# A hybrid decoder layer on one core: attention operands laid out and loaded in pieces, bias copied by head, MLP in groups of 704 columns with seven products

## The chip, the core and the metric

The kernel runs on one core of a Trainium2 chip. A core has five engines with queues of their own: TensorE (PE) for matmuls, VectorE (DVE), ScalarE (ACT), GpSimd (POOL), and SyncE (SP), which here issues the DMAs. They run side by side and wait for each other by semaphores. The metric is the device time of one execution in microseconds, as the median of several runs.

## What is computed

One decoder layer, for a prompt of 2048 tokens and 64 sample tokens, that is 2112 columns, with a model width of 1024. Cut to what matters here:

```
def decoder_layer(x, ...):
    n = rms_norm(x, ln1_g)
    proj = n @ w_in                                   # 1024 x 3360
    q, k, v = head_rms(...), head_rms(...), ...       # 8 heads x 64
    att = dilated_attention(q, k_ctx, v_ctx, ..., bias_table)   # 3 dilations
    rw, wkv_T, shift_T = rwkv7_time_mix(proj[..., 1536:], ...)
    mixed = concatenate([att, rw], -1)
    h = x + mixed @ w_out                             # 1024 x 1024
    m = rms_norm(h, ln2_g)
    y = h + square(relu(m @ w_mlp1)) @ w_mlp2         # 1024 x 4096 x 1024
```

## The kernel before, in words

Data lie transposed, features on the 128 partitions and tokens as columns. Every float32 operand is split in a high part (a copy by ScalarE to `fp32r`, helper `act`, line 184) and a low part (the difference, by VectorE, helper `tt`, line 181), and a product is three matmuls: high by high, high by low, low by high. Line 175 is the helper `stt` (scalar_tensor_tensor), line 178 `tsc`. A scheduler fixes each engine's order ahead of time from the program's order and its own estimates; tile pools with a number of buffers decide when a load may start.

The stages, by the span: up to 1208 us the projections in four groups of 512 tokens and the recurrence; 1230 to 1640 us the dilated attention, four head pairs `p` with three dilations `b` and four groups each; to 1923 us the sample tokens' attention and the output projection; then the MLP.

*Bias.* `bias_vectors` (line 458) is a generator that one loop of the projections pumps. It makes, per head, a vector by distance, and line 477 copies it to `bvD`, 128 rows for each head, four heads in one DMA. The attention reads skewed tiles `bt` of it (line 1012).

*Attention operands.* `transposed_out` writes the high and low parts of q and k of each head pair to DRAM (`qhD`, `qlD`, `khD`, `klD`, lines 831 and 832). `kq_load` (line 994) builds for each head `ty` of a pair the tiles `kst` (k high, twice), `qst` (q high above q low) and `klo` (k low, twice), 128 x 2048, from six loads of 64 x 2048 at line 1004. It is called for the first pair ahead of the attention and for the next pair at `b` = 1. Values come as tiles `vt` (line 1023). The scores are the matmuls of lines 1066 and 1067, the weighted sums those of 1091. `merge` weighs the three dilations; its weights go through DRAM (`wD`, `wrow`, lines 1166 and 1169), and a matmul with them is line 1176.

*W_out.* The 2112 columns are taken in eight tiles of `NC_` = 264; `mix_panel` (line 1306) loads and splits the mixed input (`mr`), line 1421 loads x into `h` (tile by tile of one large buffer that keeps all columns), line 1431 has the 192 matmuls of a tile, and the result is added to `h`, from which `square_sums` (line 1391) makes the norms of 128 columns at a time.

*MLP.* Two halves of 1088 and 1024 columns, in matmul chunks of 364, 362, 362 and of 512, 512. `normed(half)` scales `h` by the norms and splits it into `mmh` and `mml`. For each of eight blocks `fc` of 512 hidden units come the first layer (line 1488), relu and square, and the second layer (line 1505), which is added to `h`. `normed(1)` is called ahead of the last second layer of the first half. `mpanel` loads and splits weight panels of 128x512, with four buffers.

## Time and profile before

| | |
|---|---|
| median of 3 runs | 3410.0 us (3407.44 to 3411.9) |
| profiled execution, its own time | 3415.77 us |
| its span | 3414.0 us |
| mean granted TensorE clock | 0.974 |
| TensorE busy | 3209.2 us, 94% |
| VectorE, ScalarE, GpSimd busy | 50%, 39%, 12% |
| DMA over the span | 107 GB/s, 364.73 MB |

Times of the profile are microseconds from the span's start. Durations come from one execution, which took 5.8 us more than the median. [...] The DMA share is the mean busy share of the core's sixteen DMA engines. A wait is put down to what came last. Single operations of one engine overlap a little in the records, so the time that one costs in a row of them is read from start to start.

### The profile page before, as it was taken

The numbers are of one execution on the slowest core, as the hardware profiler recorded it, in microseconds if no ns is written. First come the engines' busy times: TensorE is split into PE (matmuls) and PEld (weight loads), VectorE is DVE, ScalarE is ACT, GpSimd is POOL, SyncE is SP. The second block draws the span as 40 slices with busy tenths as digits, with TensorE's granted clock in tenths as the row PEclk, the third lists the DMA queues.
The fourth block names the chain that finished last, engine by engine and source line by source line (L and its number), as shares of the span: only waits on it lengthen the run. The fifth ranks groups of instructions, "written<-read, shape, count | busy, mean of one in ns | idle before, by whom it ended". The sixth has DMA issues, their size and how long they took to land.

```text
span 3414.0 us, 60201 instructions
## 1 busy us (share of the span) xinstructions
PE 3209.2 (94%) x23646; PEld 2791.4 (82%) x23646; DVE 1713.4 (50%) x3951; ACT 1326.7 (39%) x3209; POOL 395.2 (12%) x713
## 2 busy tenths in 40 slices
PE   5959999999999979989899999999999999999999
PEld 5836877786788857878688899999999988888887
DVE  4635676677677525546554643333333633333333
ACT  4435564565455536657322322222222322222221
POOL 1003243342354100111000000000000000000000
PEclk9979999999999989999899999999999999999999
DMA  5445464465355495333776111111111211111112
GB/s 165 136 141 161 131 191 139 119 174 145 112 146 153 131 212 113 94 87 99 261 244 206 44 47 44 47 44 44 44 46 44 97 49 49 48 50 47 50 47 74
DMA packets 336968, 364.73 MB, mean 107 GB/s; under 512 B 112907, under 2 KB 226374, under 8 KB 333612
## 3 DMA queue, kind: packets, MB, share of 16 engines
q1 hardware_dynamic: 336684, 360.88, 36.5%
q8 instruction: 186, 3.05, 0.4%
q14 instruction: 98, 0.80, 0.1%
HBM read 286.20 MB, written 79.30 MB: 107 GB/s over the span
## 4 chain that ended last, share of the span: by engine, by line
PE 59%; DMA 6%; DVE 2%; SPq 1%; issue 1%; ACT 1%; POOL 1%; DVEq 0%; ACTq 0%; POOLq 0%
PE pm L1505 21%; PE pm L1488 21%; PE pwo L1431 4%; PE o L1091 2%; PE sc L1066 2%; PE pt L1084 2%; PE sc L1067 2%; PE pj L789 1%; DMA kst<-khD 1%; DMA vt<-vD 1%; DMA kv<-in_kc 1%; DMA mr<-mixA 1%; SPq L1421 1%; PE sc L1233 0%; DMA wD<-wh 0%
## 5 line engine op out<-in xcount | busy, mean ns | idle before, releaser
L184 ACT ACTIVATE wh<-wr 128x512 fp32r<-128x512 f32 (+1 forms) x472 | 294.3, 624 | 1027.5 <-PE pm L1505 582.3
L181 DVE TENSOR_TENSOR wl<-wr,wh 128x512 fp32r<-128x512 f32 (+1 forms) x472 | 325.9, 692 | 425.0 <-ACT wh L184 410.7
L1488 PE MATMUL pm<-mml,wh 128*128 128x512 f32 (+2 forms) x1280 | 452.5, 354 | 3.3 <-DVE mml L181 3.3
L1488 PE MATMUL pm<-mmh,wh 128*128 128x512 f32 (+2 forms) x1280 | 454.8, 356 | 0.4 <-ACT mmh L184 0.4
L1488 PE MATMUL pm<-mmh,wl 128*128 128x512 f32 (+2 forms) x1280 | 452.8, 354 | 0.0
L1505 PE MATMUL pm<-fh,wh 128*128 128x512 f32 (+2 forms) x1280 | 450.5, 355 | 0.0
L1505 PE MATMUL pm<-fh,wl 128*128 128x512 f32 (+2 forms) x1280 | 449.6, 353 | 0.0
L1505 PE MATMUL pm<-fl,wh 128*128 128x512 f32 (+2 forms) x1280 | 448.4, 352 | 0.0
L181 DVE TENSOR_TENSOR h<-pm,h 128x364 f32<-128x364 f32 (+1 forms) x320 | 190.5, 598 | 423.9 <-PE pm L1505 423.7
L1488 PEld LDWEIGHTS pm<-mml,wh 128*128 128x128 f32 x1280 | 241.0, 188 | 27.4 <-DVE mml L181 5.9
L1488 PEld LDWEIGHTS pm<-mmh,wl 128*128 128x128 f32 x1280 | 241.9, 189 | 22.5
L1505 PEld LDWEIGHTS pm<-fh,wl 128*128 128x128 f32 x1280 | 240.7, 188 | 22.4
L1488 PEld LDWEIGHTS pm<-mmh,wh 128*128 128x128 f32 x1280 | 241.4, 189 | 19.9 <-ACT mmh L184 0.9
L1505 PEld LDWEIGHTS pm<-fl,wh 128*128 128x128 f32 x1280 | 240.0, 188 | 21.5
L1505 PEld LDWEIGHTS pm<-fh,wh 128*128 128x128 f32 x1280 | 240.3, 188 | 19.2
L789 PE MATMUL pj<-wh,nh 128*128 128x256 f32 (+1 forms) x816 | 237.3, 292 | 7.5 <-ACT qn L184 3.5
L789 PE MATMUL pj<-wh,nl 128*128 128x256 f32 (+1 forms) x816 | 236.2, 290 | 1.0 <-DVE nl L181 0.9
L330 PE MATMUL pj<-nh,wh 128*128 128x512 f32 (+3 forms) x600 | 222.7, 375 | 13.2 <-ACT nh L184 9.9
L789 PE MATMUL pj<-wl,nh 128*128 128x256 f32 (+1 forms) x816 | 234.6, 288 | 0.0
L330 PE MATMUL pj<-nl,wh 128*128 128x512 f32 (+3 forms) x600 | 221.6, 370 | 3.9 <-DVE nl L181 3.8
L330 PE MATMUL pj<-nh,wl 128*128 128x512 f32 (+3 forms) x600 | 217.5, 365 | 0.0
L184 ACT ACTIVATE e<-e,st 128x256 f32<-128x256 f32 (+1 forms) x384 | 174.3, 455 | 106.3 <-DVE st L1069 104.4
(295 smaller groups left out, 6105.3 us busy)
## 6 DMA issues: line engine op xcount, KB each, us to landing
wr<-in_w SPq DMA_DIRECT2D x256, 256.0 KB
wr<-in_wr SPq DMA_DIRECT2D x120, 256.0 KB
wr<-in_wq SPq DMA_DIRECT2D x96, 256.0 KB
kv<-in_kc SPq DMA_DIRECT2D x40, 512.0 KB
kv<-in_vc SPq DMA_DIRECT2D x40, 512.0 KB
xsD<-xst SPq DMA_DIRECT2D x56, 256.0 KB
xrkv<-xsD SPq DMA_DIRECT2D x32, 384.0 KB
vt<-vD SPq DMA_DIRECT2D x48, 256.0 KB
```

The costliest lines, as they stand in the source:

```text
L181: V.tensor_tensor(out, a, b, op)
L184: S.activation(out, in_, func, bias=bias, scale=scale, **kw)
L330: PE.matmul(ps[:m, :n], a[:, k, :m], b[h * 4 + k][:, c0:c0 + n], start=(h == 0 and i == 0), stop=(h == 1 and i == 11))
L789: PE.matmul(out, a[h * 2 + k][:, i * P:i * P + m], b[:, k, :], start=(h == 0 and q == 0 and i % 2 == 0), stop=(h == 3 and q == 5 and (i % ...
L1066: PE.matmul(ps[:, c0:c0 + n], cols(qst, b, i, False), cols(kst, b, i, both), start=True, stop=False)
L1067: PE.matmul(ps[:, c0:c0 + n], cols(qst, b, i, False), cols(klo, b, i, both), start=False, stop=True)
L1084: PE.transpose(pt[:, y * P:(y + 1) * P], e[:, c0:c0 + P], ident)
L1091: PE.matmul(o[ty * 64:ty * 64 + 64, (i % 4) * P:(i % 4 + 1) * P], kv[:, ty * 64:ty * 64 + 64], ptss[ty][:, y * P:(y + 1) * P], start=fst, ...
L1421: nc.sync.dma_start(out=h[:, :, c0:c0 + NC_], in_=I["xh"][:, :, c0:c0 + NC_])
L1431: PE.matmul(ps[:, :NC_], a[k][:, o * P:(o + 1) * P], b, start=(i == 0), stop=(i == 3 * KT - 1))
L1488: PE.matmul(ps[:, :n], a[:, k], b[:, hf * 4 + k, c0:c0 + n], start=(hf == 0 and i == 0), stop=(hf == 1 and i == 11))
L1505: PE.matmul(ps[:, :n], a[:, f], b[:, c0:c0 + n], start=(i == 0), stop=(i == 11))
```

## The change

*Bias.* One DMA for each head in place of two for four heads each, with a pause of the generator after each; the generator is pumped in groups 1 and 2.

*Attention operands.* In DRAM they lie as the tiles need them: `qD` holds q high and q low, `khD` and `klD` each hold k twice, all by head pair, head, upper or lower half. 192 stores of 64x512 take the place of 64 of 128x512. A tile is loaded on all 128 partitions, for the first pair in four pieces of 512 columns, for the others in two of 1024; the loads of the next pair are pulled one at a time as the attention goes on. At the start the first bias tiles come ahead of the first keys, and the first values after the sixth piece.

*W_out.* Six tiles of 352 columns. `h` has two buffers; each finished tile is written to DRAM (`hD`), and the norms are made in tiles of 88 columns.

*MLP.* Three groups of 704 columns, two halves of 352 each. `normed(g)` reads the group back from `hD` as `hg` and makes seven operands (the four quarters' combinations by rows and columns; three are quarters and four are sums, on VectorE or GpSimd in turn). `first` takes two blocks of 128 hidden units, f and f+16, loads four weight panels, makes four sums of them on GpSimd, and does seven products of 12 matmuls; the results are combined by copies and additions, most on VectorE and two on GpSimd. The last product of a call (`late`) is finished within the next one. `second` takes four blocks of hidden units with the weights regrouped for it.

```diff
-    out["w2"] = f(inp["w_mlp2"][0].reshape(8, 4, P, 8, P).transpose(0, 3, 2, 1, 4))
+
+    out["w2"] = f(inp["w_mlp2"][0].reshape(2, 8, 2, P, 8, P).transpose(1, 4, 3, 0, 2, 5).reshape(8, 8, P, 4, P))
...
+    qD = dram.tile([4, 2, 2, 64, T], F32, name="qD")
+    khD = dram.tile([4, 2, 2, 64, T], F32, name="khD")
+    klD = dram.tile([4, 2, 2, 64, T], F32, name="klD")
...
+    hD = dram.tile([P, KT, T + NS], F32, name="hD")
...
-        for h in range(0, 8, 4):
-            nc.sync.dma_start(out=bvD[h:h + 4].rearrange("h p b n -> h p (b n)"), in_=bc(bv1[h:h + 4].rearrange("h b n -> h (b n)"), 1, P))
+        for h in range(8):
+            nc.sync.dma_start(out=bvD[h:h + 1].rearrange("h p b n -> h p (b n)"), in_=bc(bv1[h:h + 1].rearrange("h b n -> h (b n)"), 1, P))
+            yield
...
-            if g == 1:
+            if g in (1, 2):
                 next(bias, None)
...
-                nc.sync.dma_start(out=hD[h0 + pp, :, gs], in_=hi.bitcast(F32))
-                nc.sync.dma_start(out=lD[h0 + pp, :, gs], in_=lo.bitcast(F32))
+                for t, tD, xs in ((hi, hD, (0,) if isq else (0, 1)), (lo, lD, (1,) if isq else (0, 1))):
+                    for x in xs:
+                        for ty in range(2):
+                            nc.sync.dma_start(out=tD[h0 + pp, ty, x, :, gs], in_=t[64 * ty:64 * ty + 64].bitcast(F32))
...
-    def kq_load(p):
+    def kq_load(p, steps=2):
 
         kq = kqs[p % 2]
-        K = []
-        for ty in range(2):
-            rr = slice(ty * 64, ty * 64 + 64)
-            kst = kq.tile([P, T], F32R, name=f"kst{ty}", tag="kq")
-            klo = kq.tile([P, T], F32R, name=f"klo{ty}", tag="kq")
-            qst = kq.tile([P, T], F32R, name=f"qst{ty}", tag="kq")
-            for dst, src, r0 in ((kst, khD, 0), (qst, qhD, 0), (kst, khD, 64), (qst, qlD, 64), (klo, klD, 0), (klo, klD, 64)):
-                nc.sync.dma_start(out=dst[r0:r0 + 64].bitcast(F32), in_=src[p, rr])
-            K.append((kst, klo, qst))
-        return K
+        K = [[kq.tile([P, T], F32R, name=f"{nm}{ty}", tag="kq") for nm in ("kst", "klo", "qst")] for ty in range(2)]
+
+        def pieces():
+            for i in range(steps):
+                cs = slice(i * T // steps, (i + 1) * T // steps)
+                for ty in range(2):
+                    for dst, src in zip(K[ty], (khD, klD, qD)):
+                        nc.sync.dma_start(out=dst[:, cs].bitcast(F32), in_=src[p, ty].rearrange("x q t -> (x q) t")[:, cs])
+                        yield
+
+        return K, pieces()
...
-        K = ahead.pop(("kq", p))
+        K, _ = ahead.pop(("kq", p))
+        coming = iter(())
...
+                    coming = ahead["kq", p + 1][1]
...
+                    next(coming, None)
...
+        for _ in coming:
+            pass
...
-    ahead = {("kq", 0): kq_load(0)}
-    for b in range(3):
+    ahead = {("bias", 0, 0): bias_load(0, 0)}
+    ahead["kq", 0] = kq_load(0, 4)
+    for i, _ in enumerate(ahead["kq", 0][1]):
+        if i == 5:
+            vq.append(next(vgen))
+    for b in range(1, 3):
         ahead["bias", 0, b] = bias_load(0, b)
-    vq.append(next(vgen))
...
-    NC_ = 264
+    NC_ = 352
+    HT = 352
+    SQ = 88
...
+    def square_sums(h, i, c, ps, pl):
+
+        sa = pl.tile([P, 4, SQ], F32, name="sq", tag="mt2", bufs=2)
+        sb = pl.tile([P, 4, SQ], F32, name="sq", tag="mt2", bufs=2)
+        act(sa, h[:, 0:4, c:c + SQ], AF.Square)
+        act(sb, h[:, 4:8, c:c + SQ], AF.Square)
+        tt(sa, sa, sb, ALU.add)
+        tt(sa[:, :2], sa[:, :2], sa[:, 2:], ALU.add)
+        tt(sa[:, 0], sa[:, 0], sa[:, 1], ALU.add)
+        PE.matmul(ps[:SQ, 0:1], sa[:, 0], ones[:, 0:1], start=True, stop=True)
+        V.tensor_copy(ssq[i // 8][:SQ, i % 8:i % 8 + 1], ps[:SQ, 0:1])
...
-            nc.sync.dma_start(out=h[:, :, c0:c0 + NC_], in_=I["xh"][:, :, c0:c0 + NC_])
+            h = wo2.tile([P, KT, NC_], F32, name="h", bufs=2)
+            nc.sync.dma_start(out=h, in_=I["xh"][:, :, c0:c0 + NC_])
...
-                tt(h[:, o, c0:c0 + NC_], ps[:, :NC_], h[:, o, c0:c0 + NC_], ALU.add)
+                tt(h[:, o], ps[:, :NC_], h[:, o], ALU.add)
                 for _ in range(2):
                     next(sample, None)
+            nc.sync.dma_start(out=hD[:, :, c0:c0 + NC_], in_=h)
+            for i in range(NC_ // SQ):
+                square_sums(h, c0 // SQ + i, i * SQ, pst.tile([P, 512], F32, name="pst"), wo2)
...
+        def parts(w, pooled=False):
+            wh = mw.tile(list(w.shape), F32R, name="wh", tag=f"wh{w.shape[1]}", bufs=4)
+            wl = mw.tile(list(w.shape), F32R, name="wl", tag=f"wl{w.shape[1]}", bufs=4)
+            act(wh, w, AF.Copy)
+            (G if pooled else V).tensor_tensor(wl, w, wh.bitcast(F32), ALU.subtract)
+            return wh, wl
+
+        def sums_a(S, A11, A12, A21, A22):
+            G.tensor_tensor(S[0], A21, A22, ALU.add)
+            G.tensor_tensor(S[1], S[0], A11, ALU.subtract)
+            G.tensor_tensor(S[2], A11, A21, ALU.subtract)
+            G.tensor_tensor(S[3], A12, S[1], ALU.subtract)
+
+        def sums_b(E, S, B11, B12, B21, B22):
+            E.tensor_tensor(S[0], B12, B11, ALU.subtract)
+            E.tensor_tensor(S[1], B22, S[0], ALU.subtract)
+            E.tensor_tensor(S[2], B22, B12, ALU.subtract)
+            E.tensor_tensor(S[3], B21, S[1], ALU.subtract)
+
+        def normed(g):
+
+            h = hg.tile([P, KT, 2 * HT], F32, name="hg")
+            nc.sync.dma_start(out=h, in_=hD[:, :, g * 2 * HT:(g + 1) * 2 * HT])
+            rb = []
+            for c in range(2):
+                rb.append(bank())
+                for i in range(4):
+                    dg = mw.tile([P, SQ], F32, name="dg2")
+                    tsc(dg[:SQ], ident[:SQ, :SQ], rst[g][:SQ, 4 * c + i:4 * c + i + 1], None, ALU.mult, ALU.bypass)
+                    PE.matmul(rb[c][:, i * SQ:(i + 1) * SQ], ones[:SQ], dg[:SQ], start=True, stop=True)
+            mb = [[mm.tile([P, 4, HT], F32R, name=f"m{x}{i}") for x in "hl"] for i in range(7)]
+            for k in range(4):
+                q = []
+                for x in range(2):
+                    for c in range(2):
+                        t = tmp()
+                        kk = k + 4 * x
+                        stt(t, h[:, kk, c * HT:(c + 1) * HT], ln2[:, kk:kk + 1], rb[c], ALU.mult, ALU.mult)
+                        q.append(t)
+                B11, B12, B21, B22 = q
+                S = [tmp() for _ in range(4)]
+                sums_b(G if k % 2 else V, S, B11, B12, B21, B22)
+                for i, t in enumerate((B11, B21, B22, *S)):
+                    split(t, mb[i][0][:, k], mb[i][1][:, k])
+            return h, mb
+
+        def first(f, mb, late, out):
+
+            A = []
+            for x in range(2):
+                for y in range(2):
+                    wr = mw.tile([P, 4, P], F32, name="wr", tag="wr", bufs=8)
+                    nc.sync.dma_start(out=wr, in_=I["w1"][f + 16 * x, :, 4 * y:4 * y + 4])
+                    A.append(wr)
+            A11, A12, A21, A22 = A
+            S = [mw.tile([P, 4, P], F32, name="wr", tag="wr", bufs=8) for _ in range(4)]
+            sums_a(S, A11, A12, A21, A22)
+
+            def product(w, i):
+                wh, wl = parts(w, i in (2, 6))
+                bh, bl = mb[i]
+                ps = bank()
                 n = 0
+                for k in range(4):
+                    for a, b in ((wh, bh), (wh, bl), (wl, bh)):
+                        PE.matmul(ps, a[:, k], b[:, k], start=(n == 0), stop=(n == 11))
+                        n += 1
+                return ps
+
...
+            p1 = copy(product(A11, 0))
+            for step in late:
+                step()
+            relu2(0, 0, plus(product(A12, 1), p1))
+            u2 = plus(product(S[1], 4), p1)
+            p5 = copy(product(S[0], 3))
+            relu2(0, 1, plus(plus(product(S[3], 2), u2), p5, G))
+            u3 = plus(product(S[2], 5), u2)
+            relu2(1, 1, plus(u3, p5, G))
+
+            def rest():
+                relu2(1, 0, plus(product(A22, 6), u3))
+
+            return [rest]
+
+        def second(r, hs, h, last, base):
+
+            for o in range(KT):
+                wr = mw.tile([P, 4, P], F32, name="wr", tag="wr", bufs=8)
+                nc.sync.dma_start(out=wr, in_=I["w2"][r, o])
+                wh, wl = parts(wr)
+                for c in range(2):
+                    ps = bank()
+                    cs = slice(c * HT, (c + 1) * HT)
+                    i = 0
+                    for f, (fh, fl) in enumerate(hs):
+                        for a, b in ((wh, fh), (wh, fl), (wl, fh)):
+                            PE.matmul(ps, a[:, f], b[:, cs], start=(i == 0), stop=(i == 11))
+                            i += 1
+                    tt(h[:, o, cs], ps, h[:, o, cs], ALU.add)
+                if last:
+                    nc.sync.dma_start(out=O["o_y"][:, o, base:base + 2 * HT], in_=h[:, o])
+
+        for g in range(3):
+            h, mb = normed(g)
+            late = []
+            for r in range(8):
                 hs = []
...
+                for f in (2 * r, 2 * r + 1):
+                    out = [[mm.tile([P, 2 * HT], F32R, name=f"f{x}", bufs=4) for x in "hl"] for _ in range(2)]
+                    late = first(f, mb, late, out)
+                    hs.append(out)
+                for step in late:
+                    step()
+                late = []
+                hs = [hs[0][0], hs[1][0], hs[0][1], hs[1][1]]
+                second(r, hs, h, r == 7, g * 2 * HT)
```

The order of the instructions at three places. VectorE at the passage to the next half (before) or group (after). `h` and `hg` are the sums to which the last second layer adds, `wl` a weight's low part, `dg` a diagonal of norms, `mt` and `rl` scaled columns, `mml` and `ml` their low parts.

Of before:

```order
L181 TENSOR_TENSOR h<-pm_28877,h 128x362
L175 SCALAR_TENSOR_TENSOR mt_28774<-h,ln_19164,pm_28753 128x512
L181 TENSOR_TENSOR wl<-wr,wh 128x512
L178 TENSOR_SCALAR dg_28805<-ident,rst_19169 128x128
L175 SCALAR_TENSOR_TENSOR mt_28778<-h,ln_19164,pm_28753 128x512
L181 TENSOR_TENSOR h<-pm_28898,h 128x364
L178 TENSOR_SCALAR dg_28808<-ident,rst_19169 128x128
L181 TENSOR_TENSOR mml<-mt_28774,mmh 128x512
L181 TENSOR_TENSOR h<-pm_28912,h 128x362
L181 TENSOR_TENSOR mml<-mt_28778,mmh 128x512
```

Of after, the same place:

```order
L182 TENSOR_TENSOR hg<-pm,hg 128x352 x2
L179 TENSOR_SCALAR dg_27384<-ident,rst_19315 88x88
L179 TENSOR_SCALAR dg_27387<-ident,rst_19315 88x88
L1458 TENSOR_TENSOR wl<-wr,wh 128x512
L179 TENSOR_SCALAR dg_27391<-ident,rst_19315 88x88
L179 TENSOR_SCALAR dg_27394<-ident,rst_19315 88x88
L176 SCALAR_TENSOR_TENSOR rl<-hg,ln_19309,pm 128x352
L179 TENSOR_SCALAR dg_27397<-ident,rst_19315 88x88
L179 TENSOR_SCALAR dg_27400<-ident,rst_19315 88x88
L182 TENSOR_TENSOR ml_27404<-rl,mh_27403 128x352
L179 TENSOR_SCALAR dg_32428<-ident,rst_19316 88x88
L176 SCALAR_TENSOR_TENSOR rl<-hg,ln_19309,pm 128x352 x3
```

Before, the next half's scalings stand among the additions of the second layer; after, they begin behind the last of these.

SyncE at the start of the attention: `kst`, `qst`, `klo` are the first pair's operands, `bt` the bias, `wr` weight panels of the projection, `vD` and `out_o_vwin` its stores.

Of before:

```order
L868 DMA out_o_vS<-qnS 64x256
L1004 DMA kst_14628<-khD 64x2048
L1004 DMA qst_14630<-qhD 64x2048
L1004 DMA kst_14628<-khD 64x2048
L1004 DMA qst_14630<-qlD 64x2048
L1004 DMA klo_14629<-klD 64x2048 x2
L1004 DMA kst_14637<-khD 64x2048
L871 DMA vD<-qn 128x2x256
L872 DMA out_o_vwin<-qn 128x2x256
L1004 DMA qst_14639<-qhD 64x2048
```

Of after:

```order
L315 DMA wr<-in_wq 128x512 x2
L1018 DMA bt_14762<-bvD 128x256
L1018 DMA bt_14764<-bvD 128x256
L1009 DMA kst_14766<-khD 128x512
L876 DMA vD<-qn 128x2x256
L877 DMA out_o_vwin<-qn 128x2x256
L1009 DMA klo_14767<-klD 128x512
L1009 DMA qst_14768<-qD 128x512
L315 DMA wr<-in_wq 128x512
L1009 DMA kst_14769<-khD 128x512
L1009 DMA klo_14770<-klD 128x512
L1009 DMA qst_14771<-qD 128x512
```

The two bias tiles and the first pieces of the operands moved ahead of the projection's last two panels.

GpSimd within a pair of calls of `first` (lines 1462 to 1465 are the four sums of weight panels, 1458 the low part of a panel, 1533 an addition of products). Before, GpSimd has nothing there.

```order
L1462 TENSOR_TENSOR wr<-wr 128x512
L1458 TENSOR_TENSOR wl<-wr,wh 128x512
L1463 TENSOR_TENSOR wr<-wr 128x512
L1464 TENSOR_TENSOR wr<-wr 128x512
L1465 TENSOR_TENSOR wr<-wr 128x512
L1458 TENSOR_TENSOR wl<-wr,wh 128x512
L1533 TENSOR_TENSOR rl<-rl 128x352 x2
L1458 TENSOR_TENSOR wl<-wr,wh 128x512 x2
L1533 TENSOR_TENSOR rl<-rl 128x352 x2
```

The next call's sums stand between the splits of the one before.

## Rows read from the trace of the kernel before

**Rows 1.** The page's first part: busy us (share of the span) xinstructions of each engine.

```profile
PE 3209.2 (94%) x23646; PEld 2791.4 (82%) x23646; DVE 1713.4 (50%) x3951; ACT 1326.7 (39%) x3209; POOL 395.2 (12%) x713
```

**Rows 2.** Windows: us; busy (xcount) of each engine; TensorE clock, DMA share, GB/s.

```profile
216.00:220.00 4.00, 0.00 (x0) 0.00 (x0) 0.00 (x0) 0.00 (x0) 0.00 (x0) 0.93 0.26 106
...
1210.00:1220.00 10.00, 0.77 (x2) 0.47 (x2) 0.00 (x0) 0.00 (x0) 0.00 (x0) 0.65 1.02 246
1240.00:1270.00 30.00, 26.61 (x220) 21.71 (x220) 13.83 (x65) 20.73 (x70) 0.00 (x0) 1.00 1.03 219
1360.00:1370.00 10.00, 1.91 (x9) 1.73 (x11) 1.10 (x5) 0.17 (x1) 0.00 (x0) 0.50 0.62 129
1460.00:1470.00 10.00, 0.61 (x5) 0.37 (x4) 0.00 (x0) 1.63 (x6) 0.00 (x0) 0.78 0.76 171
1660.00:1720.00 60.00, 53.94 (x497) 44.31 (x490) 29.85 (x84) 9.70 (x23) 0.00 (x0) 0.91 0.97 319
```

**Rows 3.** SyncE's timeline around the bias copies and the residual's loads: start, us, instruction.

```profile
205.00 21.99 SPq L313 DMA_DIRECT2D wr<-in_wr  x1
...
1681.04 18.67 SPq L1421 DMA_DIRECT2D h<-in_xh  x8
```

**Rows 4.** What TensorE waited for, 204 to 245 us: total, times, longest.

```profile
PE pj L468 <- DMA oh<-in_soneh: 27.5, 1, 27.5
```

**Rows 5.** The chain that ended last, in order of time: start us, us, what.

```profile
1194.52 0.39 SPq L836
...
1216.73 13.57 DMA bt<-bvD
...
1460.22 8.27 DMA wD<-wh
...
1886.61 18.36 PE pwo L1431 x150
...
2131.37 47.79 PE pm L1488 x288
...
2750.56 43.95 PE pm L1505 x192
```

**Rows 6.** Windows in the MLP, columns as in group 2.

```profile
1922.70:1988.02 65.32, 58.63 (x315) 54.44 (x314) 48.67 (x106) 31.69 (x64) 2.01 (x1) 0.92 0.20 61
1926.70:1934.70 8.00, 7.13 (x24) 6.20 (x24) 7.93 (x18) 4.06 (x9) 0.00 (x0) 0.50 0.49 155
1945.00:2658.00 713.00, 712.30 (x4295) 711.70 (x4295) 281.25 (x512) 171.91 (x324) 2.01 (x1) 1.00 0.15 45
2657.00:2706.61 49.61, 49.61 (x306) 49.61 (x305) 38.96 (x72) 15.46 (x27) 0.00 (x0) 1.00 0.36 122
```

**Rows 7.** VectorE's timeline at the end of W_out and the first normalization.

```profile
1901.31 0.69 DVE L181 TENSOR_TENSOR sq<-sq 128x512 f32<-128x512 f32 x1
...
1905.12 0.16 DVE L1403 COPY ssq<-pst 128x1 f32<-128x1 f32 x1 [1.64 <-PE pst L1402]
...
1938.79 0.61 DVE L175 SCALAR_TENSOR_TENSOR mt<-h,ln,pm 128x384 f32<-128x384 f32 x1
1939.32 0.55 DVE L181 TENSOR_TENSOR mml<-mt,mmh 128x384 fp32r<-128x384 f32 x1
1939.79 0.53 DVE L181 TENSOR_TENSOR fl<-rl,fh 128x364 fp32r<-128x364 f32 x1
```

**Rows 8.** Groups by line and shape: busy us, mean ns, idle before and its releasers.

```profile
L1179 POOL TENSOR_TENSOR ob<-ob,ob 128x512 f32<-128x512 f32 x24 | 30.7, 1277 | 175.1 <-DVE ob L181 143.3 <-issue 29.2 <-ACT e L184 2.6
...
L181 DVE TENSOR_TENSOR wl<-wr,wh 128x512 fp32r<-128x512 f32 x120 | 83.1, 693 | 129.7 <-ACT wh L184 129.6
```

**Rows 9.** Timelines of GpSimd and VectorE at 423 us, in the projections.

```profile
423.15 0.23 POOL L567 TENSOR_TENSOR xt<-xt,itmp 128x30 f32<-128x30 f32 x1
...
423.78 0.67 POOL L567 TENSOR_TENSOR xt<-xt,itmp 128x29 f32<-128x29 f32 x1
...
423.67 0.69 DVE L181 TENSOR_TENSOR wl<-wr,wh 128x512 fp32r<-128x512 f32 x1
```

More of the change, by code (lines that the diff above doesn't have):

```diff
@@ L820, in transposed_out @@
             gg = gq if isq else gk
-            hD, lD = (qhD, qlD) if isq else (khD, klD)
+            hD, lD = (qD, qD) if isq else (khD, klD)
             h0 = (cp % 2) * 2
@@ L1365, in _build @@
     ph2.close()
[L1366 removed]
+    for nm, t in (("mixR", mixR), ("mixA", mixA)):
         if nm in dbg:
@@ L1380, in _build @@
     for t in ssq:
         V.memset(t, 1.0)
-    def mpanel(src):
-        wr = mw.tile([P, 4, P], F32, name="wr", tag="wr", bufs=4)
-        nc.sync.dma_start(out=wr, in_=src)
-        wh = mw.tile([P, 4, P], F32R, name="wh", tag="wh", bufs=4)
-        wl = mw.tile([P, 4, P], F32R, name="wl", tag="wl", bufs=4)
-        split(wr, wh, wl)
-        return wh, wl
-    def square_sums(i, ps, pl):
-        c0 = i * P if i < 9 else 1088 + (i - 9) * P
-        m = NS if i == 8 else P
-        sa = pl.tile([P, 4, P], F32, name="sq", tag="mt2", bufs=2)
-        sb = pl.tile([P, 4, P], F32, name="sq", tag="mt2", bufs=2)
-        act(sa[:, :, :m], h[:, 0:4, c0:c0 + m], AF.Square)
-        act(sb[:, :, :m], h[:, 4:8, c0:c0 + m], AF.Square)
-        tt(sa[:, :, :m], sa[:, :, :m], sb[:, :, :m], ALU.add)
-        tt(sa[:, :2, :m], sa[:, :2, :m], sa[:, 2:, :m], ALU.add)
-        tt(sa[:, 0, :m], sa[:, 0, :m], sa[:, 1, :m], ALU.add)
-        PE.matmul(ps[:m, 0:1], sa[:, 0, :m], ones[:, 0:1], start=True, stop=True)
-        V.tensor_copy(ssq[i // 9][:m, i % 9:i % 9 + 1], ps[:m, 0:1])
-        if i in (8, 16):
-            q = ssq[i // 9]
+    def square_sums(h, i, c, ps, pl):
[8 more added lines that the diff above has]
+        V.tensor_copy(ssq[i // 8][:SQ, i % 8:i % 8 + 1], ps[:SQ, 0:1])
+        if i % 8 == 7:
+            q = ssq[i // 8]
@@ L1413, in _build @@
             wo_panel(kqb.tile([P, T], F32R, name="wo", tag="kq"), k)
-        tile_ = 0
-        ends = [(i + 1) * P for i in range(8)] + [1088 + i * P for i in range(9)]
         order = (4, 5, 6, 7, 0, 1, 2, 3)
@@ L1432, in _build @@
                         i += 1
-                tt(h[:, o, c0:c0 + NC_], ps[:, :NC_], h[:, o, c0:c0 + NC_], ALU.add)
+                tt(h[:, o], ps[:, :NC_], h[:, o], ALU.add)
                 for _ in range(2):
                     next(sample, None)
-            while tile_ < 17 and ends[tile_] <= c0 + NC_ < NT:
-                square_sums(tile_, pst.tile([P, 512], F32, name="pst"), wo2)
-                tile_ += 1
+            nc.sync.dma_start(out=hD[:, :, c0:c0 + NC_], in_=h)
+            for i in range(NC_ // SQ):
+                square_sums(h, c0 // SQ + i, i * SQ, pst.tile([P, 512], F32, name="pst"), wo2)
@@ new lines, in _build, with bank, tmp, relu2 @@
+    with pool(name="mm", bufs=1, side="right") as mm, pool(name="hg", bufs=2, side="right") as hg, pool(name="pm", bufs=8, space=PSUM) as pm:
+        def bank():
+            return pm.tile([P, 512], F32, name="pm")[:, :HT]
+        def parts(w, pooled=False):
[14 more added lines that the diff above has]
+            E.tensor_tensor(S[3], B21, S[1], ALU.subtract)
+        def tmp():
+            return mw.tile([P, HT], F32, name="rl", bufs=12)
+        def normed(g):
[37 more added lines that the diff above has]
+                ps = bank()
+                n = 0
+                for k in range(4):
[3 more added lines that the diff above has]
+                return ps
+            def relu2(x, c, t):
+                stt(t, t, 0.0, t, ALU.max, ALU.mult)
+                fh, fl = out[x]
+                split(t, fh[:, c * HT:(c + 1) * HT], fl[:, c * HT:(c + 1) * HT])
+            def plus(a, b, E=V):
+                t = tmp()
+                E.tensor_tensor(t, a, b, ALU.add)
+                return t
+            def copy(a):
+                t = tmp()
+                act(t, a, AF.Copy)
+                return t
+            p1 = copy(product(A11, 0))
[30 more added lines that the diff above has]
+            for r in range(8):
+                hs = []
+                for f in (2 * r, 2 * r + 1):
[7 more added lines that the diff above has]
+                second(r, hs, h, r == 7, g * 2 * HT)
```

76 lines of the change are left out of this document (3 added, 73 removed).

## The prediction

> **What bounds the kernel now.** The page comes first: TensorE is busy 3209 of 3414 us [rows 1], so time can only come from its idle stretches, from fewer or cheaper matmuls, or from the clock. Next the windows, to see where TensorE isn't full [rows 2]: at 216 us nothing computes while the DMA engines are busy at 0.26 of their time and move 106 GB/s; at 1210, 1360 and 1460 TensorE has 0.77, 1.91 and 0.61 of 10 us. SyncE's timeline then says who stands in the way at 205 us: one weight load takes 22 us to issue, behind the two copies of line 477 [rows 3]. The waits give TensorE's price for it, 27.5 us in one piece [rows 4]. The chain names the same for the attention (a bias tile that lands at 1230.3, a store that takes 8.27 us) and shows W_out and MLP as unbroken TensorE work, from which the price of a matmul is read [rows 5]. [...]
>
> **Matmul price.** 47.79 us / 288 = 165.9 ns at a mean of 362.7 columns, 43.95 / 192 = 228.9 at 512, 18.36 / 150 = 122.4 at 264 [rows 5]. Between the neighbours 264 and 362.7, 352 columns cost 161.3 ns.
>
> **MLP matmuls, -74.** Before: 16 x 47.79 + 16 x 43.95 = 1467.8 us. After: first layer 3 groups x 16 x 7 products x 12 = 4032, second layer 3 x 8 x 8 x 2 x 12 = 4608, together 8640 x 0.1613 = 1393.6. That lies on TensorE, which is full, so all of it counts, if the operands come in time.
>
> **MLP side work, +15 (0 to +90).** One call of `first` lasts 84 x 0.1613 = 13.55 us on TensorE. GpSimd gets four sums and two splits of 128x512 at 1.28 us and two adds of 352 columns, by columns 0.9 each [rows 8]: 9.5 us. VectorE gets five splits at 0.69 [rows 8], four squarings and four subtractions at about 0.5 by the starts in [rows 7] and five adds from PSUM at 0.5: 10 us. ScalarE has less. Each engine alone fits. But they don't run independently: a GpSimd op of 30 columns takes 0.23, the one of 29 that starts at 423.78 takes 0.67 and ends at 424.45, just after VectorE's split of 423.67 to 424.36 [rows 9]. So ops with two SBUF operands on the two engines hold each other up, here by 0.44 us. Four panels of lookahead (7.7 us of matmuls) cover single delays; 15 us is 0.6 per pair of `first`, one such delay.
>
> [...]
>
> **Group boundaries, +68 (+40 to +90).** `normed` of the next half stood among the adds of the last second layer, two to five ops between them; `normed(1)` and `normed(2)` now stand behind the last add, on all engines. Nothing is left to cover them. VectorE then has 16 scalings, 28 subtractions and 8 sums of 352 columns. At 384 columns one op starts 0.53 (scaling) and 0.47 (subtraction) after the other [rows 7]; the 32 columns less are worth 0.03: 16 x 0.50 + 36 x 0.44 = 23.8. Eight small scalings (0.2), two panel splits and about 4 us for GpSimd's eight sums (8 x 0.9, half of it in VectorE's way) make 31. Meanwhile TensorE, whose order takes the first four products by quarters, can do 42 matmuls, 6.8 us. Loss 24.5 a time, twice 49; the clock falls with such a pause, as at the start of the MLP [rows 6], where 8 us at half speed cost 4: I take 2.5 each, 5. At the first group the same work follows four `square_sums` of the last chunk, which wait for two buffers; VectorE's part of one is 1.25 us, from its add at 1901.31 to its copy at 1905.28 [rows 7] lie 4.0 with other work: I take 2.1 each, 8.5. So 33 in place of the 65.3 - 47.8 = 17.5 of before [rows 6]: +15.5. The old half boundary (49.61 - 47.79 = 1.8) goes [rows 5, 6]. 49 + 5 + 15.5 - 1.8 = 68. The low end is without GpSimd's part and with the matmuls that could be done earlier, the high end with GpSimd's sums wholly in the way and 4.0 per `square_sums`.
>
> **Bias copy, -28 (-12 to -37).** Two copies of 2304 KB become eight of a quarter, spread over the pumps. The DMA share of 0.26 says that four of sixteen engines moved the old ones [rows 2]; the load behind them waited 22 us and TensorE 27.5 [rows 3, 4]. At the 319 GB/s of a load on all engines [rows 2] 4.7 MB take 15 us, 1.8 a head, behind which one weight panel can wait unnoticed. [...] The upper end is the whole idle stretch of 205 to 243 us, the lower that the copies still run on four engines but in pieces.
>
> [...]
>
> **Attention operands, -38 (-15 to -52), extra stores +3 (0 to +20).** The loads of one head pair are 6.29 MB in 64-partition pieces at 219 GB/s with all engines busy (1.03), 28.7 us; loads of 128 partitions run at 319 with no more share (0.97) [rows 2], 19.7 us, which I take for the new ones. At the front the matmuls wait from 1210 until the bias lands at 1230.3 [rows 2, 5]: now the bias tiles, the first pieces of keys and queries and the first values stand among the projection's last panels. I take 17 of 20 us; what is left is the other pieces (4.7 MB, 15 us) ahead of the later values. At 1360 and 1460 the stores and loads of the merge weights (`wD`, 8.27 us [rows 5]) stand behind a burst of keys and queries. The new pieces still stand as a burst in nearly the same place; it is 9 us shorter. For three such places, one of them too short for a row here, 7 each: 21. The low end is that only the front moves, the high end all stalls. The 128 more stores at 0.39 us of issue each [rows 5] are 50 us of SyncE, spread over four groups in a stage where SyncE isn't last; a few may delay a panel.
>
> **W_out, -7 (-14 to +10).** 1536 x 0.1224 = 188.0 becomes 1152 x 0.1613 = 185.8, -2. The eight issues of `xh` at once, 18.7 us of SyncE [rows 3], become two ahead; two tiles fewer wait for their first panel: -5. Against it each write of `hD` waits on SyncE for VectorE's last add, with the panels two tiles on queued behind it; the panels of the next tile are ahead of it, so I count nothing, and up to +10.
>
> **Sum.** -74 + 15 + 68 - 28 - 38 + 3 - 7 = -61. The profiled execution took 3415.8 us, 5.8 over the median of 3410.0: 3354.8 there, 3349 as a median.
>
> **Rivals.**
> (1) *The two engines' lock decides the first layer*: slower. If VectorE's ops with two SBUF operands (7.5 us per `first`) and GpSimd's 9.5 exclude each other wholly, a `first` takes 17.0 us, a pair 34.0 against 27.1 of matmuls: 24 x 6.9 = +166 for +15, 3500. Over a pair with its second layer the two have 39.5 us in 58.1, so it needs that little is done ahead; four panels are little. It decides from 3.2 us of stall per pair on (15 + 61 = 76). Against it: only some ops overlap, and the panels of the second layer let the next sums start early. 10%.
> (2) *Boundaries and stalls at the high end*: +90 and +50, 3406, no change. For it speaks that GpSimd's sums come on top at each. 7%.
> (3) *The loads come no earlier*: the bursts still stand ahead of `wD` and the values, and the copies still hold panels: attention and copy at 12 each, 3391. 10%.
> (4) *All of it hidden*: attention -52, copy -37, no stall, boundaries +55: 3298. The lookahead speaks for it, the order of VectorE's work against it. 15%.
> My forecast, 3349 (3315 to 3385), has 58%.
>
> **The numbers.** The range 3290 to 3405 holds the forecast, (3), most of (4), little of (2), none of (1): 0.83. A measurement of this kernel tells about 0.2%, 7 us, from no change. Faster: 0.58 + 0.15 + 0.10 and 0.03 of (2), 0.86. Within: 0.04 of (2). Slower: (1), 0.10.
>
> **What would show it.** Matmuls of 352 columns at 161 ns, 8640 of them; TensorE over 0.97 busy between boundaries, else (1), seen in VectorE's and GpSimd's ops longer than in [rows 8]. Three gaps in TensorE of about 33, 25 and 25 us, with VectorE busy, and a lower clock behind them. No idle stretch at 216; under 5 us at the front of attention; 128-partition loads above 300 GB/s. If the gaps are under 15 us the forecast is too high; if `first` lasts over 15 us it falls.

## The result, and the profile after

The changed kernel takes 3377.66 us (median, 3371.13 to 3380.98), before 3410.58; the ratio is 0.990 with a 95% interval of 0.9888 to 0.9913. It is faster by 33 us. The forecast was a gain of 61, to 3349 us; the measured time is 29 above it and still inside the stated range. In its profiled execution the span is 3379.2 us and the granted clock 0.958 (before 0.974). Of its page, TensorE's busy share is that of [rows 1], on fewer microseconds; VectorE and GpSimd have much more to do:

```profile
PE 3185.7 (94%) x24250; PEld 2865.0 (85%) x24250; DVE 2144.6 (63%) x4576; ACT 1474.0 (44%) x3491; POOL 946.2 (28%) x1122
...
PE 66%; DVE 7%; DMA 6%; ACT 2%; SPq 2%; issue 2%; POOL 1%; POOLq 0%; ACTq 0%; DVEq 0%
```

The windows that answer to [rows 2] (us; busy of each engine; clock, DMA share, GB/s):

```profile
216.00:220.00 4.00, 1.13 (x18) 0.59 (x13) 3.93 (x11) 0.15 (x1) 0.12 (x1) 1.00 1.09 321
1210.00:1220.00 10.00, 10.00 (x82) 10.00 (x81) 0.75 (x1) 1.98 (x3) 0.00 (x0) 0.94 0.80 201
1240.00:1270.00 30.00, 27.79 (x212) 22.65 (x210) 13.44 (x61) 19.05 (x64) 0.00 (x0) 0.89 0.91 316
1330.00:1360.00 30.00, 30.00 (x254) 24.93 (x253) 21.13 (x89) 23.61 (x81) 1.27 (x1) 1.00 0.65 218
1360.00:1370.00 10.00, 10.00 (x53) 7.64 (x52) 6.20 (x22) 6.19 (x21) 2.42 (x3) 1.00 0.16 54
1460.00:1470.00 10.00, 10.00 (x69) 8.36 (x67) 6.30 (x22) 5.91 (x20) 2.37 (x2) 1.00 0.08 30
```

At 216 us the DMA engines are now all busy (share 1.09 in place of 0.26) and move 321 GB/s in place of 106, and from 205 to 243 us TensorE is busy for 31.3 of 38 us in place of 4.5. At 1240 the operands come at 316 GB/s in place of 219. The window of 1210 is full, but with the projection, which ends later: the chain of the attention starts no earlier. The window 1330 to 1360, with a burst in it, is full too, at a DMA share of 0.65; the pauses at 1360 and 1460 are gone. Those were waits for the merge weights. Between the first and the last weighted sum before has two of them, 21.3 us in all, and the changed kernel has none:

```profile
PE ax L1176 <- DMA wrow<-wD: 21.3, 2, 10.8
```

The MLP in the chain of waits (start us, us, what) answers to [rows 5]:

```profile
2371.42 30.73 PE pm L1568 x192
...
2402.18 0.53 DVE hg L182
...
2427.62 5.91 DVE ml L182 x9
...
2440.30 15.00 PE pm L1522 x92
2455.30 30.71 PE pm L1568 x192
2486.02 26.88 PE pm L1522 x168
```

12 x 14 matmuls of 352 columns take 26.88 us, 192 take 30.71: 160.0 ns each. Between 2402.15, where the second layer ends, and 2455.30, where the first pair of the next group does, lie 53.15 us of which a pair needs 26.88. The steps there are VectorE's low parts (`ml`) and scalings (`rl`). Windows of that passage, columns as above:

```profile
2402.15:2455.30 53.15, 43.78 (x185) 35.95 (x185) 52.02 (x89) 25.04 (x51) 24.33 (x19) 0.71 0.33 106
2410.00:2420.00 10.00, 7.17 (x19) 4.45 (x18) 10.00 (x18) 5.29 (x11) 4.38 (x4) 0.50 0.52 186
2420.00:2430.00 10.00, 7.98 (x18) 4.87 (x18) 10.00 (x20) 5.29 (x11) 3.14 (x3) 0.50 0.00 0
```

From 2410 to 2430 VectorE is busy in every microsecond, and TensorE sits at a granted clock of 0.50, half of full speed, and gets through 19 and 18 matmuls in 10 us, where at 160.0 ns each 62 would fit.

Placed by the same marks in both traces (the last weighted sum of the attention starts, W_out ends, the MLP ends):

| | before | after | difference |
|---|---|---|---|
| first weighted sum of the attention | 1236.1 | 1236.4 | 0 |
| last one | 1639.0 | 1607.4 | -31.6 |
| W_out ends | 1922.7 | 1901.3 | -21.4 |
| MLP ends | 3409.8 | 3375.5 | -34.3 |

So of the copy and the attention 31.6 us arrived where 63 were forecast (28 + 38 - 3), W_out gave back 10, and the MLP gained 13. These marks come from one trace each. The start of the first weighted sum lies between 1228.4 and 1236.4 us in six traces of kernels whose projections have the same code (the changed kernel, e11, e4, e6, e7 and e8 below), so a difference of under 8 us in it says nothing.

### The profile page after: what moved, and what is told of

Read it like the earlier page. It is cut to its first block, busy times and chain, and to the rows that moved or that the text cites. A ratio compares the mean times of both kernels' runs of the same rounds, so it can differ in the third digit from the quotient of the medians.

```text
span 3379.2 us, 63833 instructions
## 1 busy us (share of the span) xinstructions
PE 3185.7 (94%) x24250; PEld 2865.0 (85%) x24250; DVE 2144.6 (63%) x4576; ACT 1474.0 (44%) x3491; POOL 946.2 (28%) x1122
## 4 chain that ended last, share of the span: by engine, by line
PE 66%; DVE 7%; DMA 6%; ACT 2%; SPq 2%; issue 2%; POOL 1%; POOLq 0%; ACTq 0%; DVEq 0%
PE pm L1568 22%; PE pm L1522 18%; PE pwo L1434 5%; PE pj L792 3%; PE pj L332 3%; PE o L1099 3%; PE pt L1092 2%; PE sc L1074 2%; PE sc L1075 2%; DVE ml L182 1%; DMA mr<-mixA 1%; DVE rl L176 1%; DVE wl L182 1%; DMA raw<-in_wo 1%; PE pu L658 1%
## 5 line engine op out<-in xcount | busy, mean ns | idle before, releaser
L185 ACT ACTIVATE wh<-wr 128x512 fp32r<-128x512 f32 x744 | 464.3, 626 | 881.6 <-PE pm L1568 523.9
L1568 PE MATMUL pm<-fh,wl 128*128 128x352 f32 x1536 | 494.7, 322 | 0.0
L1568 PE MATMUL pm<-fl,wh 128*128 128x352 f32 x1536 | 491.0, 322 | 0.0
L1568 PE MATMUL pm<-fh,wh 128*128 128x352 f32 x1536 | 491.0, 322 | 0.0
L1522 PE MATMUL pm<-mh,wh 128*128 128x352 f32 x1344 | 445.3, 332 | 17.1 <-ACT mh L185 16.7
L1522 PE MATMUL pm<-ml,wh 128*128 128x352 f32 x1344 | 444.9, 332 | 9.8 <-DVE ml L182 9.7
L1522 PE MATMUL pm<-mh,wl 128*128 128x352 f32 x1344 | 442.4, 329 | 0.9 <-DVE wl L1458 0.6
L1458 DVE TENSOR_TENSOR wl<-wr,wh 128x512 fp32r<-128x512 f32 x432 | 356.0, 824 | 2.6
L1522 PEld LDWEIGHTS pm<-mh,wh 128*128 128x128 f32 x1344 | 258.1, 192 | 31.3 <-ACT mh L185 31.2
L1522 PEld LDWEIGHTS pm<-ml,wh 128*128 128x128 f32 x1344 | 258.7, 193 | 15.7 <-DVE ml L182 14.9
L1522 PEld LDWEIGHTS pm<-mh,wl 128*128 128x128 f32 x1344 | 259.4, 193 | 2.4 <-DVE wl L1458 2.3
```

Source lines behind the costliest of these rows:

```text
L185: S.activation(out, in_, func, bias=bias, scale=scale, **kw)
L1458: (G if pooled else V).tensor_tensor(wl, w, wh.bitcast(F32), ALU.subtract)
L1522: PE.matmul(ps, a[:, k], b[:, k], start=(n == 0), stop=(n == 11))
L1568: PE.matmul(ps, a[:, f], b[:, cs], start=(i == 0), stop=(i == 11))
```

## The experiments

Times are medians beside runs of the kernel before on the same chip; the ratio is to those, with its 95% interval.

**The three parts alone.** The edits are the hunks of the change: the copy by head with the pumping in groups 1 and 2 (e1), the new layout with its stores and loads (e2), W_out and MLP (e3).

> The kernel before with the bias copy by head alone. In the changed kernel the projections are 30 us ahead of before at 250 us and 12 us behind at their end, so about 45 us were given back between. Theory A, the new order of the projections' and the recurrence's instructions, which comes with the copy in pieces, gives it back (smaller pauses, lower granted clock): 3395 to 3412 us, the idle piece at 216 us gone, TensorE's clock lower between 250 and 1200 us than before (0.985), the attention at the same time as before. Theory B, the 128 more stores of the attention's operands give it back: here nothing is given back, 3378 to 3385 us.

Measured 3392.2 against 3414.1, 0.9927 (0.9912 to 0.9942).

> The kernel before with the attention's operands laid out and loaded as in the changed kernel, alone. Theory A (order after the bias copy): the projections end as before, the attention gains its 40 us: 3365 to 3375 us. Theory B (stores): the projections lose 30 to 45 us between 250 and 1200 us, which eats the gain of the attention: 3400 to 3415 us.

Measured 3397.4, 0.9945 (0.9925 to 0.9965).

> The kernel before with W_out and MLP of the changed kernel, alone. From the two traces: MLP 13 us shorter, W_out and the sample attention 10 longer: 3400 to 3412 us. If the three parts add up, this and the two other parts' differences sum to -33 us; if the projections lose by their order as such, any of the three may lose there.

Measured 3412.6, 0.9990 (0.9979 to 1.0001).

The parts give -22, -17 and -1.5, together -40, close to the whole's -33 (-38 in a second measurement, below). e1 and e2 both lie between the ranges of the two theories. The layout gives 17 of the 35 that were priced, and there theory B is the nearer. The first weighted sum comes at 1222 in e1 (14 us earlier than before) and at 1250 in e2 (14 later): at that mark the layout has spent what the copy saved.

Where e1 loses a part of its gain can be followed by the reductions of the recurrence, 18 in each kernel (operation, count, ns min/median/max, first and last start; before, then e1):

```profile
L603 POOL TENSOR_TENSOR rs<-var,mhalf x18: 1635/1650/2101, 331.5 to 1184.1; 128x8 f32<-128x8 f32 x18
```

```profile
L604 POOL TENSOR_TENSOR rs<-var,mhalf x18: 1625/1646/2023, 292.1 to 1156.5; 128x8 f32<-128x8 f32 x18
```

The lead is 39 us at the first and 28 at the last, and half of those 28 go between there and the first weighted sum. In e1 loads of the first pair's operands, still of 64 partitions, stand on SyncE ahead of the last stores of k and of panels for the projection. One window (before, then e1) and two pieces of e1's chain show it:

```profile
1180.00:1210.00 30.00, 23.40 (x185) 22.76 (x183) 9.48 (x18) 8.14 (x15) 7.35 (x4) 0.94 0.81 214
```

```profile
1180.00:1210.00 30.00, 14.04 (x76) 13.09 (x77) 2.19 (x4) 4.44 (x8) 0.00 (x0) 0.61 1.01 250
```

```profile
1177.48 15.69 DMA qst<-qhD
1193.23 13.08 DMA khD<-qhi
```

**Stores alone (e5).** The new layout and its stores, with the old loads in their old place:

```
-            for dst, src, r0 in ((kst, khD, 0), (qst, qhD, 0), (kst, khD, 64), (qst, qlD, 64), (klo, klD, 0), (klo, klD, 64)):
-                nc.sync.dma_start(out=dst[r0:r0 + 64].bitcast(F32), in_=src[p, rr])
+            for dst, src, r0 in ((kst, khD, 0), (qst, qD, 0), (kst, khD, 64), (qst, qD, 64), (klo, klD, 0), (klo, klD, 64)):
+                nc.sync.dma_start(out=dst[r0:r0 + 64].bitcast(F32), in_=src[p, ty, r0 // 64])
```

> The kernel before with the new layout in DRAM and its 192 stores of 64x512, but the loads as before (six of 64x2048 a head, before the bias tiles). With layout alone the projections ended 23 us later and the first weighted sum of the attention came 14 us later than before, where 17 earlier were forecast. Theory: the stores (twice the writes for k, 64 partitions each) hold up SyncE's queue and the weight panels: here the first weighted sum comes 10 to 30 us later than before's 1247 and the time is 3425 to 3440. Rival: the new place of the first loads, among the projection's last panels, does it: here no change, 3408 to 3418.

Measured 3440.6 against 3414.5, 1.0077 (1.0062 to 1.0092): 26 us slower, and the first weighted sum 25 us later (1261.1; before has it at 1236.1, and the 1247 of the expectation is in no view). The rival falls. With e2 it also gives the price of the loads: 3397 - 3441 is -43. What a store costs on SyncE is in the view of its line, first in before, then in the changed kernel (operation, count, ns min/median/max, first and last start):

```profile
L831 SPq DMA_DIRECT2D khD<-qhi x16: 319/332/1555, 442.1 to 1192.5; - x16
```

```profile
L837 SPq DMA_DIRECT2D khD<-qhi x64: 445/592/1468, 428.3 to 1214.7; - x64
```

A store from 64 partitions takes 592 ns to issue in the median, one from 128 takes 332; between 300 and 1219 us of the span all stores of these operands took 25 us of SyncE before and 118 in the changed kernel.

That the stores cost 26 us is shown; that they cost it by holding up weight panels, as the theory has it, is not. ScalarE, the first to use a panel, waits less for panels of the projections than before (300 to 1190 us: what waits for what, us in total, times, longest; before, then e5):

```profile
ACT wh L184 <- DMA wr<-in_wq: 34.9, 20, 3.4
ACT wh L184 <- DMA wr<-in_wr: 32.6, 14, 6.4
```

```profile
ACT wh L184 <- DMA wr<-in_wq: 29.4, 19, 4.6
ACT wh L184 <- DMA wr<-in_wr: 15.8, 6, 6.0
```

What does change in this stretch is the clock (before, then e5):

```profile
300.00:1190.00 890.00, 844.52 (x8550) 698.79 (x8548) 603.53 (x1197) 498.22 (x1144) 321.97 (x577) 0.98 0.51 146
```

```profile
300.00:1190.00 890.00, 840.48 (x8412) 694.08 (x8410) 590.53 (x1179) 491.96 (x1127) 313.07 (x573) 0.96 0.56 148
```

TensorE is busy for 4 us less, and the granted clock is 0.96 for 0.98, which on 890 us is some 18 us by my estimate. The scheduler's order differs too: in e5 the twelfth of the reductions `rs` starts at 855.9 us, before at 921.6. Whether the stores cost by their time on SyncE or by the order that the scheduler makes of them, no run tells for certain.

**By number or by bytes.** The rows of the layout interleaved, so that a store covers 128 partitions again, and the loads don't change:

```
-    khD = dram.tile([4, 2, 2, 64, T], F32, name="khD")
+    khD = dram.tile([4, 2, 64, 2, T], F32, name="khD")
...
-                        for ty in range(2):
-                            nc.sync.dma_start(out=tD[h0 + pp, ty, x, :, gs], in_=t[64 * ty:64 * ty + 64].bitcast(F32))
+                        nc.sync.dma_start(out=tD.rearrange("p t q x n -> p (t q) x n")[h0 + pp, :, x, gs], in_=t.bitcast(F32))
...
-                        nc.sync.dma_start(out=dst[:, cs].bitcast(F32), in_=src[p, ty].rearrange("x q t -> (x q) t")[:, cs])
+                        nc.sync.dma_start(out=dst[:, cs].bitcast(F32), in_=src[p, ty].rearrange("q x t -> (q x) t")[:, cs])
```

> The changed kernel with the rows of its DRAM layout interleaved: each head's tile holds row q of the first and of the second operand next to each other, so that a store is again one DMA of 128x512 (96 in place of 192 of 64x512, the same bytes), and the loads are as in the changed kernel. The stores alone cost 26 us in the kernel before. If what costs is their number on SyncE's queue (0.59 us each): half of it comes back or more, 3377 - 15 to 22 = 3355 to 3362. If it is the doubled bytes of k: nothing comes back, 3372 to 3382.

> The kernel before with the layout alone (3397 with the 192 stores), rows interleaved in the same way. By number of stores: 3375 to 3383, the first weighted sum of the attention 10 us or more earlier than with 192 stores (1261). By bytes: 3392 to 3402.

> The changed kernel once more, beside the two others on the same chip: 3370 to 3382.

Measured, against 3412.2 (the 1261 of e10's expectation is e5's mark; with the layout alone, e2, it is 1250.1): the changed kernel again (e11) 3374.6, 0.9890 (0.9872 to 0.9908); with interleaved rows (e9) 3356.3, 0.9838 (0.9823 to 0.9852); the layout alone with interleaved rows (e10) 3369.2, 0.9877 (0.9852 to 0.9901), 43 below before, where 17 were measured with 192 stores. That is more than e10's expectation had, and all of the loads' -43: nothing of the stores' price is left. The same bytes are written, so it isn't the bytes. The number of stores, their 64 partitions, and the order of all engines changed together, and were not tried apart. Their row in the layout alone:

```profile
L833 SPq DMA_DIRECT2D khD<-qhi x32: 319/424/1127, 445.8 to 1223.3; - x32
```

In e9 a store of `khD` takes 424 ns of SyncE in the median too, so the 96 stores of e9 take some 41 us by my estimate, in place of 118. The first weighted sum comes at 1221.5 in e10 and at 1250.1 in e2. So the whole of the gain is made ahead of the attention: from there to the last weighted sum e10 has 376.5 us and e2 372.9, and the loads have not become cheaper. An early recurrence alone isn't the price either: the twelfth `rs` starts at 844.1 in e9 and at 843.4 in the changed kernel, and e9 has its first weighted sum 29 us earlier (1207.5).

**The passage between groups (e4).**

```
-            h, mb = normed(g)
+            h, mb = nxt
...
+                if r == 7 and g < 2:
+                    nxt = normed(g + 1)
                 second(r, hs, h, r == 7, g * 2 * HT)
```

> The changed kernel with the next group's normalization called ahead of the last second layer of a group, as before did at its half. Theory: the two gaps of 26 us at the passages are VectorE's work with nothing to cover it, and the last second layer (30.7 us of TensorE, 13 of VectorE) can cover most of it: 3377 - 45 = 3332 us (3325 to 3342), passages under 5 us each. [...]

Measured 3357.8 against 3414.1, 0.9826 (0.9806 to 0.9845), 17 to 20 below the changed kernel. The time lies 16 us above the top of the expected range, 3342. Whether GpSimd's sums hold up VectorE within the second layer was not tried apart. The window over the last pair and second layer of a group and the first of the next, in e4:

```profile
2809.96:2941.99 132.03, 124.33 (x739) 120.40 (x738) 109.46 (x178) 49.79 (x97) 53.58 (x40) 0.96 0.28 86
```

It lasts 132.0 us where two rounds need 115.2: 16.8 are lost in place of 26.3, twice. VectorE is busy 109 of 132 us, and without a break in the middle, where its order alternates `normed` with what the second layer needs:

```profile
2870.00:2880.00 10.00, 8.89 (x55) 8.31 (x53) 10.00 (x23) 3.67 (x8) 0.01 (x1) 1.00 0.59 204
2880.00:2890.00 10.00, 8.31 (x28) 6.43 (x29) 10.00 (x14) 5.54 (x12) 7.94 (x7) 0.66 0.12 44
```

**The sums of weight panels on VectorE (e8).** All four operations of `sums_a`, of which the first stands here:

```
-            G.tensor_tensor(S[0], A21, A22, ALU.add)
+            V.tensor_tensor(S[0], A21, A22, ALU.add)
...
```

> The changed kernel with the four sums of weight panels on VectorE in place of GpSimd. VectorE then has 10 + 4 x 0.62 = 12.5 us per call of first, 13.4 on TensorE, and GpSimd 4.4 in place of 9.5. In the changed kernel VectorE's splits take 824 ns in the mean against 693 before, with no pause on TensorE. [...]

Measured 3375.4 against 3414.5, 0.9890 (0.9865 to 0.9915): the time of the changed kernel. Groups by shape between 1998 and 2371 us (busy us, mean ns, idle before), the changed kernel ahead, then e8:

```profile
L1458 DVE TENSOR_TENSOR wl<-wr,wh 128x512 fp32r<-128x512 f32 x118 | 97.4, 825 | 0.7
L182 DVE TENSOR_TENSOR fl<-rl,fh 128x352 fp32r<-128x352 f32 x53 | 45.1, 850 | 5.6 <-ACT fh L185 3.9
L1533 POOL TENSOR_TENSOR rl<-rl 128x352 f32<-128x352 f32 x28 | 36.5, 1305 | 34.8 <-DVE rl L1533 34.8
```

```profile
L1458 DVE TENSOR_TENSOR wl<-wr,wh 128x512 fp32r<-128x512 f32 x118 | 80.9, 686 | 0.7
L182 DVE TENSOR_TENSOR fl<-rl,fh 128x352 fp32r<-128x352 f32 x55 | 42.4, 770 | 5.7 <-ACT fh L185 4.0
```

The splits fall from 825 to 686 ns, as in [rows 8] (693), and TensorE has nothing of it: what the two engines take from each other doesn't reach TensorE, whose chain in this stretch is matmuls alone in both kernels (in e8 it was read from 1990 to 2300 us). That the panels done ahead are what covers it is argued, not shown. That GpSimd is held up beside VectorE is plainest where VectorE works without a break, at the first group (start us, us, engine, line), GpSimd ahead:

```profile
1918.09 1.28 POOL L1464 TENSOR_TENSOR wr<-wr 128x512 f32<-128x512 f32 x1
1919.32 5.91 POOL L1465 TENSOR_TENSOR wr<-wr 128x512 f32<-128x512 f32 x1
```

```profile
1919.77 0.51 DVE L1468 TENSOR_TENSOR rl<-rl 128x352 f32<-128x352 f32 x1
1920.20 1.28 DVE L1458 TENSOR_TENSOR wl<-wr,wh 128x512 fp32r<-128x512 f32 x2
1921.40 0.51 DVE L1469 TENSOR_TENSOR rl<-rl 128x352 f32<-128x352 f32 x1
1921.84 0.51 DVE L1470 TENSOR_TENSOR rl<-rl 128x352 f32<-128x352 f32 x1
1922.28 1.38 DVE L182 TENSOR_TENSOR ml<-rl,mh 128x352 fp32r<-128x352 f32 x3
1923.58 0.51 DVE L1471 TENSOR_TENSOR rl<-rl 128x352 f32<-128x352 f32 x1
1924.02 2.04 DVE L176 SCALAR_TENSOR_TENSOR rl<-hg,ln,pm 128x352 f32<-128x352 f32 x4
```

A sum of 128x512 that takes 1.28 us at 1918.09 takes 5.91 from 1919.32 on, while VectorE runs one op with two SBUF operands after the other, and ends at 1925.23, 1.14 after the last of these (1923.58 + 0.51). The four scalings that follow (1924.02 to 1926.06), with one operand in PSUM, don't hold it. So in this place GpSimd's sum lasted through a whole row of VectorE's ops, 5.91 us for 1.28.

**Width of W_out's tiles.** `NC_` = 264 in the changed kernel (e6), and in e4 (e7):

> The changed kernel with W_out in tiles of 264 columns again (all else as changed: two buffers, writes of h to DRAM). From the sample attention to the end of W_out the changed kernel lost 10 us against before, and the kernel with W_out and MLP alone 14. Theory: the wider tiles do it (fewer and longer tiles wait for their panels): 3362 to 3369. Rival: the writes of h and the loads behind them on SyncE do it: 3374 to 3382.

> Both at once: the next group's normalization ahead of the last second layer, and W_out in tiles of 264. If the two add up: 3358 - 12 = 3346. If the wider tiles are not the cause: 3355 to 3360.

Measured 3367.8 (0.9869, 0.9850 to 0.9888) and 3353.8 (0.9839, 0.9810 to 0.9867), against 3414.5. By time the first is 7 to 10 us better than the changed kernel, and the second isn't told from e4 (0.9826); the intervals overlap. The stage itself tells more. From the last weighted sum (1601.2) to the end of W_out (1888.4) e6 has 287.2 us, the changed kernel 293.9, before 283.7. Taken to the start of W_out's last matmul, the six kernels with tiles of 352 columns have 293.5 to 297.1, and the three with 264 columns and the rest of the new W_out 284.7 to 290.4. So the width takes some 7 of the 10 us.

With either width TensorE waits 10 to 13 us for the weights of the last merge; in the kernels that keep the old W_out and MLP it waits under 1. In the changed kernel, 1600 to 1640 us:

```profile
PE sc L1187 <- DMA wrow<-wD: 12.1, 1, 12.1
```

The weights don't come later: the first matmul with them starts 18.4 us after the start of the last weighted sum before (1657.37) and 13.3 after it in the changed kernel (1620.74). Before has the sample tokens' attention on TensorE in that time, with waits of its own, where the new order has it later, among W_out's tiles. The two stretches, from the last weighted sum to W_out's first matmul and from there to its last (before, then the changed kernel):

```profile
1639.00:1672.20 33.20, 23.23 (x210) 10.38 (x208) 25.77 (x68) 7.09 (x15) 0.00 (x0) 0.60 0.85 286
1672.20:1922.40 250.20, 243.44 (x2561) 224.08 (x2552) 111.80 (x367) 59.49 (x138) 2.18 (x1) 1.00 0.63 202
```

```profile
1607.40:1630.70 23.30, 8.52 (x33) 3.57 (x30) 16.67 (x31) 6.07 (x12) 0.00 (x0) 0.64 0.45 148
1630.70:1900.90 270.20, 260.18 (x2359) 229.59 (x2360) 123.75 (x401) 63.04 (x142) 3.29 (x2) 0.96 0.78 258
```

TensorE's idle time in the first stretch is 14.8 us in place of 10.0, so the wait of 12.1 costs some 5 net. In the second it is 10.0 in place of 6.8, at a clock of 0.96 in place of 1.00. Why the scheduler has the sample attention later was not tried apart.

**All that helped, together (e12).** Interleaved rows, `normed` ahead of the last second layer, tiles of 264.

> All three that helped, together: next group's normalization ahead of the last second layer, W_out in tiles of 264 columns, interleaved rows. If they add up: 3354 - 18 = 3336 (3328 to 3346). If the projections' order eats it: 3350.

Measured 3331.7 (3327.24 to 3333.84) against 3412.2, 0.9765 (0.9749 to 0.9781): 80 us faster than before, 43 faster than the changed kernel. The gains add up, to within the spread.

## Why the prediction was right in sign and half in size

| term | forecast | measured | from |
|---|---|---|---|
| bias copy | -28 | -22 | e1 |
| attention's loads | -38 | -43 | e2 less e5 |
| extra stores | +3 | +26 | e5 |
| W_out | -7 | +10 | stage marks |
| MLP matmuls | -74 | -85 | 8640 x 0.1600 = 1382.4 |
| MLP side work | +15 | 0 | chain |
| passages | +68 | +72 | chain |

*Stores.* The term that failed. It priced 128 stores at the 0.39 us of another store in [rows 5], one of 128 partitions, and then let SyncE's time be free because SyncE wasn't last. The stores took 93 us more of SyncE, not 50, and 26 us of the kernel's time, more than the range's +20. That SyncE wasn't last in the stage was true and settled nothing. By which way the time arrives stays open: as a lower clock and another order, not as the delayed panels that the prediction allowed for.

*Bias copy.* All sixteen engines (share 1.09 at 216 us, 321 GB/s) and no long pause, as forecast. The four engines of before are an estimate, 0.26 x 16 = 4.2; that a copy by head would reach all sixteen was not shown before it ran. No run shows the -28 as such: nearest is the wait of 27.5 us [rows 4], and e1 shows 31 us at the place: in e1 the recurrence's first output starts at 222 us, before at 253. 22 are left, within the range. That the order at the end of the projections changes with the copy, and with it where the first pair's loads stand, was not in the sum.

*Attention.* The burst did shrink, with 316 GB/s for 219. From the first to the last weighted sum 31.9 us went where 21 were priced, 7 for each of three stalls: the waits for the merge weights went as a whole. So the third rival, loads that come no earlier, fell. The front, priced at 17, didn't move in the changed kernel, for with its stores the projection ends later; e2 has it 11 earlier than e5.

*W_out.* The wrong sign. The prediction counted two waits fewer for a first panel, and nothing for the width of a tile or for the order of the sample attention around it. The width took some 7 us. The rest lies with the sample attention, which no longer stands where TensorE waits for the merge's weights.

*MLP.* The price of a matmul at 352 columns lies below the line between its neighbours, 160.0 for 161.3. The first rival, that VectorE and GpSimd decide the first layer, fell: the two engines do hold each other up (5.91 us for a sum of 1.28 on GpSimd, splits of 825 ns for 686 on VectorE), and TensorE didn't wait for it between the passages: the chain from 1998.98 to 2371.42 is matmuls alone, with 26.88 and 30.71 us in turn.

*Passages.* 39.9 - 17.5 + 26.3 + 25.3 - 1.8 = 72: each close to its forecast (33, 25, 25), with VectorE as the cause and a clock of 0.50 beside it. The first is longer; its chain also goes through loads of weight panels and GpSimd's sums, but with these sums on VectorE (e8) it is no shorter, 40.7. That nearly all of it could be won back by the order of calls, as e4's theory had it, was wrong: a third could, for VectorE had no room left (busy in all of the 20 us from 2870).

Stores and W_out are 40 us worse than priced and the copy 6; matmuls (-11), side work (-15), passages (+4) and loads (-5) together are 27 better. e3 measures -1.5 where W_out and MLP together were priced at +2, by terms that miss in opposite directions. So that the time stayed within the range is in part luck: two terms beyond or at the end of their own ranges were half paid for by an MLP that came cheaper than priced. The terms as measured give -42. The whole was measured at -33 and -38, so 4 to 9 us stay unplaced; the order of the projections differs in each of these kernels.
